# Cross entropy with label smoothing: a first row in three transfers, a second row in eleven, eight of which follow into its buffers

## The chip, the cores and the metric

The kernel runs on one core of a Trainium2 chip. The metric is the device time of one execution in microseconds (us). A profiled execution also has a span, from its first to its last instruction; here it is some 1.8 to 2.2 us shorter than the time.

The engines are named as in the profile: PE multiplies matrices, ACT computes exponentials and logarithms, DVE is the vector engine, POOL is the general engine beside it, and SP issues most of the loads. SBUF and PSUM are the two on-chip memories in which the tiles lie. At the end PE turns the 128 results of a row into one line (a transpose); matmuls without a use of their own, the "warming" ones, run before the last two transposes.

## The reference

```python
batch, num_classes = 256, 32000          # logits float32, labels int32, smoothing 0.1
log_probs = logits - max(logits, axis=-1)
log_probs = log_probs - log(sum(exp(log_probs), axis=-1))
targets   = smoothing / num_classes everywhere, plus 1 - smoothing at the label
out       = -sum(targets * log_probs, axis=-1)        # 256 values
```

256 rows on 128 partitions are two rows per partition, "row 0" and "row 1". For each row the kernel needs the sum of the logits (DVE), the sum of their exponentials (ACT), the label's logit (a gather), and at the end a logarithm. All 32.77 MB must be loaded once.

## The kernel before

A row is loaded in tiles. DVE and ACT both work on a tile when it has landed. DVE sums the first and second half in one instruction with two inputs; ACT writes its exponentials to a scratch tile that nobody reads and keeps the sum, which a second short instruction (ACTIVATION_READ_ACCUMULATOR) then writes out.

```python
WIDTHS = (
    (8000, 8000, 8000, 8000),
    (8000, 6272, 4736, 3648, 2688, 2048, 1536, 1216, 1024, 832),
)
TURN_MAX = 3648
...
    def sum_logits(xt, w: int, out: bass.AP):
        h = w // 2
        jd = junk.tile([P, max(WIDTHS[0]) // 2], FP32, name="jd", tag="jd")
        return nc.vector.scalar_tensor_tensor(
            out=jd[:, :h], in0=xt[:, :h], scalar=1.0, in1=xt[:, h:w],
            op0=ALU.mult, op1=ALU.add, accum_out=out)

    def sum_exps(xt, w: int, out: bass.AP) -> None:
        if w > TURN_MAX:
            ja = junk.tile([P, max(WIDTHS[0])], BF16, name="ja", tag="ja")   # one scratch tile
        else:
            ja = turn.tile([P, TURN_MAX], BF16, name="jt", tag="jt")         # three in turn
        nc.scalar.activation(out=ja[:, :w], in_=xt[:, :w], func=AF.Exp, accum_out=out)
...
        # after row 0: halve the partial sums on POOL until one is left, then the logarithm on ACT
        while n > 1:
            n //= 2
            half = small.tile([P, 2, n], FP32, ...)
            nc.gpsimd.tensor_tensor(out=half[:], in0=sums[:, :, :n], in1=sums[:, :, n:], op=ALU.add)
            sums = half
        nc.scalar.activation(out=lse[:], in_=sums[:, 1, :], func=AF.Ln)
...
    elast = psum.tile([P, 1], FP32, name="elast", tag="elast")   # row 1: sum of the last tile
    ...
    nc.scalar.activation(out=lse[:], in_=elast[:], func=AF.Ln, bias=done[2][:, 1:2])
```

The softmax here doesn't subtract the row's maximum and nothing guards it: scores larger than these inputs give would overflow.

Of the kernel before, what the change touches and what calls it, by code (L numbers as in the profile page):

```python
# [8 lines left out]
FP32 = mybir.dt.float32  # L9
BF16 = mybir.dt.bfloat16  # L10
I32 = mybir.dt.int32
ALU = mybir.AluOpType
AF = mybir.ActivationFunctionType
# [1 line left out]


WIDTHS = (
    (8000, 8000, 8000, 8000),
    (8000, 6272, 4736, 3648, 2688, 2048, 1536, 1216, 1024, 832),
)  # L20

RING_MIN = 4736

TURN_MAX = 3648

WARM_LEFT, WARM_COLS = 5, 256

# [32 lines left out]
def kernel(  # L60
# [7 lines left out]
    nc = tc.nc  # L68
    nc.at_finalize(_issue_first_transfers_at_start)
    B, C = logits.shape  # L70
    P = nc.NUM_PARTITIONS
    R = B // P
# [4 lines left out]
    c_small = eps / float(C)  # L77
    c_big = 1.0 - eps

    ring = ctx.enter_context(tc.tile_pool(name="ring", bufs=3))  # L80
    tail = ctx.enter_context(tc.tile_pool(name="tail", bufs=1))
    junk = ctx.enter_context(tc.tile_pool(name="junk", bufs=1))
    turn = ctx.enter_context(tc.tile_pool(name="turn", bufs=3))
    small = ctx.enter_context(tc.tile_pool(name="small", bufs=1))

    psum = ctx.enter_context(
        tc.tile_pool(name="psum", bufs=1, space=bass.MemoryType.PSUM)
    )

    tbl = _exp_ln_table(nc.m.arch)  # L90
    if tbl is not None:
        nc.scalar.add_instruction(  # L92
            mybir.InstLoadActFuncSet(
                name=nc.get_next_instruction_name(),
# [7 lines left out]
    x = logits.rearrange("(p r) c -> p (r c)", r=R)  # L102
# [3 lines left out]
        out=lab[:], in_=labels.bitcast(I32).rearrange("(p f) -> p f", p=P)  # L106
    )
    rowoff = small.tile([P, R], I32, name="rowoff", tag="rowoff")
    for r in range(R):
        nc.gpsimd.iota(  # L110
            out=rowoff[:, r : r + 1],
# [6 lines left out]
        out=flat_idx[:],  # L118
        in0=rowoff[:],
        in1=lab[:].rearrange("p (r two) -> p r two", two=2)[:, :, 0:1],  # L120
        op=ALU.add,
    )
    gat = small.tile([P, R], FP32, name="gat", tag="gat")
    for r in range(R):
        nc.gpsimd.indirect_dma_start(  # L125
            out=gat[:, r : r + 1],
            out_offset=None,
            in_=logits[:],
# [12 lines left out]
    weighted = [  # L141
        small.tile([P, 1], FP32, name=f"weighted{r}", tag=f"weighted{r}")[:]
        for r in range(R - 1)
    ] + [xsum[:, 0:1]]
    for r in range(R):
        nc.gpsimd.tensor_scalar(  # L146
            out=weighted[r],
            in0=gat[:, r : r + 1],
# [4 lines left out]

    res = small.tile([1, P, R], FP32, name="res", tag="res")

    def load(w: int, col: int, name: str):
        if w >= RING_MIN:
            xt = ring.tile([P, max(WIDTHS[0])], FP32, name="xt", tag="xt")
        else:
            xt = tail.tile([P, w], FP32, name=name, tag=name)  # L160
        if col == 0:

            h = w // 2
            nc.sync.dma_start(out=xt[:, :h], in_=x[:, :h])
            nc.scalar.dma_start(out=xt[:, h:w], in_=x[:, h:w])
        else:
            nc.sync.dma_start(out=xt[:, :w], in_=x[:, col : col + w])  # L167
        return xt

    def sum_logits(xt, w: int, out: bass.AP):  # L170
# [3 lines that stand above are left out]
            out=jd[:, :h],  # L174
            in0=xt[:, :h],
            scalar=1.0,
            in1=xt[:, h:w],
            op0=ALU.mult,
            op1=ALU.add,
            accum_out=out,  # L180
        )

    def sum_exps(xt, w: int, out: bass.AP) -> None:
        if w > TURN_MAX:
            ja = junk.tile([P, max(WIDTHS[0])], BF16, name="ja", tag="ja")
        else:
            ja = turn.tile([P, TURN_MAX], BF16, name="jt", tag="jt")
        nc.scalar.activation(out=ja[:, :w], in_=xt[:, :w], func=AF.Exp, accum_out=out)  # L188

    def row_of(column: bass.AP, name: str):  # L190

        row = psum.tile([1, P], FP32, name=name, tag=name)
        nc.tensor.transpose(out=row[:], in_=column, identity=ident[:])  # L193
        return row

    col = 0
    for r in range(R - 1):
        n = len(WIDTHS[r])
        sums = small.tile([P, 2, n], FP32, name=f"sums{r}", tag=f"sums{r}")
        for t, w in enumerate(WIDTHS[r]):  # L200
            xt = load(w, col, f"xl{r}_{t}")
            col += w
            sum_logits(xt, w, sums[:, 0, t : t + 1])
            sum_exps(xt, w, sums[:, 1, t : t + 1])


        while n > 1:
            assert n % 2 == 0
            n //= 2
            half = small.tile([P, 2, n], FP32, name=f"half{r}_{n}", tag=f"half{r}_{n}")  # L210
            nc.gpsimd.tensor_tensor(  # L211
                out=half[:], in0=sums[:, :, :n], in1=sums[:, :, n:], op=ALU.add
            )
            sums = half
        lse = small.tile([P, 1], FP32, name=f"lse{r}", tag=f"lse{r}")
        nc.scalar.activation(out=lse[:], in_=sums[:, 1, :], func=AF.Ln)  # L216
        lin = small.tile([P, 1], FP32, name=f"lin{r}", tag=f"lin{r}")
        nc.gpsimd.tensor_tensor(out=lin[:], in0=sums[:, 0, :], in1=weighted[r], op=ALU.add)
        scaled = small.tile([P, 1], FP32, name=f"scaled{r}", tag=f"scaled{r}")
        nc.gpsimd.tensor_scalar(  # L220
            out=scaled[:], in0=lin[:], scalar1=-c_small, scalar2=None, op0=ALU.mult
        )
        loss = small.tile([P, 1], FP32, name=f"loss{r}", tag=f"loss{r}")
        nc.gpsimd.tensor_tensor(out=loss[:], in0=scaled[:], in1=lse[:], op=ALU.add)  # L224
        loss_t = row_of(loss[:], f"loss_t{r}")
        nc.vector.tensor_copy(out=res[:, :, r : r + 1], in_=loss_t[:])  # L226
# [2 lines left out]

    r = R - 1  # L230
    n = len(WIDTHS[r])
    elast = psum.tile([P, 1], FP32, name="elast", tag="elast")
    pairs = [
        small.tile([P, 2], FP32, name=f"pair{i}", tag=f"pair{i}") for i in range(2)
    ]
# [3 lines left out]
    warm = psum.tile([P, WARM_COLS], FP32, name="warm", tag="warm")  # L239
    for t, w in enumerate(WIDTHS[r]):  # L240
        left = n - 1 - t
        xt = load(w, col, f"xl{r}_{t}")
        col += w
        part = sum_logits(
            xt, w, xsum[:, t + 1 : t + 2] if left > 1 else pairs[1 - left][:, 0:1]
        )
        if left == 0:
            sum_exps(xt, w, elast[:])
        elif left <= 2:
            sum_exps(xt, w, pairs[2 - left][:, 1:2])  # L250
        else:
            sum_exps(xt, w, esum[:, t : t + 1])
        if left == 2:
            with tc.issue_after(part.ins):
                nc.vector.tensor_reduce(
                    out=done[0][:, 0:1], in_=xsum[:, : t + 2], axis=AX.X, op=ALU.add
                )
                nc.vector.tensor_reduce(
                    out=done[0][:, 1:2], in_=esum[:, :t], axis=AX.X, op=ALU.add
                )  # L260
        elif left < 2:
            i = 1 - left
            nc.vector.tensor_tensor(  # L263
                out=done[i + 1][:], in0=done[i][:], in1=pairs[i][:], op=ALU.add
            )
        if left == WARM_LEFT:


            for i in range(w // WARM_COLS):
                nc.tensor.matmul(  # L270
                    warm[:],
                    lhsT=ident[:],
                    rhs=xt[:, i * WARM_COLS : (i + 1) * WARM_COLS],
                    start=True,
                    stop=True,
                )

    lse = small.tile([P, 1], FP32, name=f"lse{r}", tag=f"lse{r}")
# [6 lines left out]
        out=res[:, :, r : r + 1],  # L285
        in0=lin_row[:],
        scalar=-c_small,
        in1=lse_t[:],
# [4 lines left out]
        out=out.rearrange("(g i) -> g i", g=1), in_=res[:].rearrange("g p r -> g (p r)")  # L293
# [36 lines left out]
```

## Time and profile before

| What | Value |
|---|---|
| Time, median | 84.79 us (84.74 to 84.87, 6 runs) |
| Span of the profiled run | 83.2 us |
| Busy: ACT, DVE, POOL | 58.8, 37.1, 5.7 us |
| Idle of ACT before the first tile of row 1 | 1.75 us |
| Start of the last logarithm | 80.20 us |

The prediction below shows the chain of waits and ACT's timeline. The lines of a timeline give start, duration, engine, line, operation, tiles, and in brackets how long the engine had been idle and who released it.

```profile
45.07 0.08 DVE L173 DVE_READ_ACCUMULATOR jd<-xt 128x1 f32 x1
...
47.85 0.20 POOL L211 TENSOR_TENSOR half<-sums 128x4 f32<-128x4 f32 x1 [28.18 <-ACT ja L188]
48.12 0.19 POOL L211 TENSOR_TENSOR half<-half 128x2 f32<-128x2 f32 x1
```

DVE had finished its tile at 45.15 and didn't start the next before 50.32 (but for a small copy at 49.62). POOL's additions, 0.20 and 0.19 us, fall in that pause, so their durations are those of a POOL beside which DVE does nothing.

### The profile page before, as it was taken

The numbers are of one execution on the slowest core, as the hardware profiler recorded it, in microseconds if no ns is written. First come the engines' busy times: TensorE is split into PE (matmuls) and PEld (weight loads), VectorE is DVE, ScalarE is ACT, GpSimd is POOL, SyncE is SP. The second block draws the span as 40 slices with busy tenths as digits, with TensorE's granted clock in tenths as the row PEclk, the third lists the DMA queues.
The fourth block names the chain that finished last, engine by engine and source line by source line (L and its number), as shares of the span: only waits on it lengthen the run. The fifth ranks groups of instructions, "written<-read, shape, count | busy, mean of one in ns | idle before, by whom it ended". The sixth has DMA issues, their size and how long they took to land.

```text
span 83.2 us, 230 instructions
## 1 busy us (share of the span) xinstructions
PE 7.0 (8%) x23; PEld 5.0 (6%) x23; DVE 37.1 (45%) x35; ACT 58.8 (71%) x31; POOL 5.7 (7%) x19
## 2 busy tenths in 40 slices
PE   0000000000000000000000010000000000899020
PEld 0000000000000000000000000000000000787000
DVE  0000005950495009910397017922944736754860
ACT  5000005997499809994399908997999999999960
POOL 3201640031000000000000040000000000000000
PEclk9999999999999999999999999999999999999995
DMA  5999999997999899989998998998999999999600
GB/s 131 416 416 408 454 423 462 477 447 323 477 493 431 369 431 493 446 369 416 493 462 354 416 439 386 495 447 370 428 420 414 442 407 415 412 414 412 256 0 0
DMA packets 2258, 32.77 MB, mean 394 GB/s; under 512 B 337, under 2 KB 338, under 8 KB 850
## 3 DMA queue, kind: packets, MB, share of 16 engines
q1 hardware_dynamic: 2018, 30.72, 87.4%
q10 hardware_dynamic: 144, 2.05, 5.8%
q0 software_dynamic: 96, 0.00, 0.1%
HBM read 32.77 MB, written 0.00 MB: 394 GB/s over the span
## 4 chain that ended last, share of the span: by engine, by line
DMA 64%; ACT 32%; issue 1%; SPq 0%; PE 0%; DVE 0%; ACTq 0%
DMA xt<-in_logits_dram 40%; DMA xl<-in_logits_dram 23%; ACT ja L188 17%; ACT jt L188 15%; SPq L167 0%; PE lse_t L193 0%; DVE res L284 0%; ACT lse L279 0%; ACTq L188 0%
## 5 line engine op out<-in xcount | busy, mean ns | idle before, releaser
L188 ACT ACTIVATE ja<-xt 128x8000 bf16<-128x8000 f32 (+2 forms) x7 | 43.9, 6276 | 20.1 <-DMA xt<-in_logits_dram 20.0
L173 DVE SCALAR_TENSOR_TENSOR jd<-xt 128x4000 f32<-128x4000 f32 (+2 forms) x7 | 27.7, 3954 | 33.6 <-DMA xt<-in_logits_dram 33.6
L188 ACT ACTIVATE jt<-xl 128x3648 bf16<-128x3648 f32 (+6 forms) x7 | 12.2, 1748 | 0.1
L173 DVE SCALAR_TENSOR_TENSOR jd<-xl 128x1824 f32<-128x1824 f32 (+6 forms) x7 | 7.9, 1125 | 5.2 <-DMA xl<-in_logits_dram 5.0
L270 PE MATMUL warm<-xl,ident 128*128 128x256 f32 x20 | 6.1, 471 | 21.4 <-DMA xl<-in_logits_dram 21.4
L270 PEld LDWEIGHTS warm<-xl,ident 128*128 128x128 f32 x20 | 4.8, 246 | 22.5 <-DMA xl<-in_logits_dram 21.7
L193 PE MATMUL loss_t<-ident,loss 128*1 128x128 f32 x1 | 0.4, 372 | 49.2 <-POOL loss L224 49.2
L193 PEld LDWEIGHTS loss_t<-ident,loss 128*1 128x1 f32 x1 | 0.1, 79 | 49.2 <-POOL loss L224 49.2
L226 DVE COPY res<-loss_t 1x128 f32<-1x128 f32 x1 | 0.3, 278 | 4.5 <-PE loss_t L193 4.5
L211 POOL TENSOR_TENSOR half<-sums 128x4 f32<-128x4 f32 x1 | 0.2, 198 | 28.2 <-ACT ja L188 28.2
L125 POOL DMA_INDIRECT gat<-in_logits_dram,flat_idx x2 | 2.0, 1004 | 0.7 <-POOL ident masks.py:199 0.4
L92 ACT ACT_TABLE_LOAD x1 | 1.3, 1283 | 0.9 <-PEq L311 0.9
L188 ACT ACTIVATION_READ_ACCUMULATOR ja<-xt 128x1 f32 x7 | 1.3, 186 | 0.0
L188 ACT ACTIVATION_READ_ACCUMULATOR jt<-xl 128x1 f32 x7 | 1.3, 181 | 0.0
L146 POOL TENSOR_SCALAR weighted<-gat 128x1 f32<-128x1 f32 x1 | 0.8, 763 | 5.8 <-DMA gat<-in_logits_dram,flat_idx 5.8
L105 POOL DMA_DIRECT2D lab<-in_labels_dram x1 | 0.8, 766 | 1.0 <-POOLq L311 1.0
L216 ACT ACTIVATE lse<-half 128x1 f32<-128x1 f32 x1 | 0.2, 203 | 0.6 <-POOL half L211 0.6
L173 DVE DVE_READ_ACCUMULATOR jd<-xt 128x1 f32 x7 | 0.6, 82 | 0.0
L173 DVE DVE_READ_ACCUMULATOR jd<-xl 128x1 f32 x7 | 0.6, 82 | 0.0
L117 POOL TENSOR_TENSOR flat_idx<-rowoff,lab 128x2 int32<-128x2 int32 x1 | 0.2, 197 | 5.4 <-DMA lab<-in_labels_dram 5.4
L193 PE MATMUL lin_t<-ident,done 128*1 128x128 f32 x1 | 0.3, 270 | 3.0 <-DVE done L263 3.0
L282 DVE COPY lin_row<-lin_t 1x128 f32<-1x128 f32 x1 | 0.3, 278 | 0.4 <-PE lin_t L193 0.4
(20 smaller groups left out, 3.8 us busy)
## 6 DMA issues: line engine op xcount, KB each, us to landing
xt<-in_logits_dram SPq DMA_DIRECT2D x4, 4000.0 KB, 21.1
xt<-in_logits_dram SPq DMA_DIRECT2D x1, 3136.0 KB, 19.4
xt<-in_logits_dram SPq DMA_DIRECT2D x1, 2368.0 KB
xt<-in_logits_dram SPq DMA_DIRECT2D x1, 2000.0 KB, 11.5
xt<-in_logits_dram ACTq DMA_DIRECT2D x1, 2000.0 KB, 13.2
xl<-in_logits_dram SPq DMA_DIRECT2D x1, 1824.0 KB, 19.5
xl<-in_logits_dram SPq DMA_DIRECT2D x1, 1344.0 KB, 22.3
xl<-in_logits_dram SPq DMA_DIRECT2D x1, 1024.0 KB, 24.3
```

What stands on the lines that cost most here:

```text
L92: nc.scalar.add_instruction(mybir.InstLoadActFuncSet(name=nc.get_next_instruction_name(), act_func_set_id=tbl, ins=[], outs=[],))
L105: nc.gpsimd.dma_start(out=lab[:], in_=labels.bitcast(I32).rearrange("(p f) -> p f", p=P))
L117: nc.gpsimd.tensor_tensor(out=flat_idx[:], in0=rowoff[:], in1=lab[:].rearrange("p (r two) -> p r two", two=2)[:, :, 0:1], op=ALU.add,)
L125: nc.gpsimd.indirect_dma_start(out=gat[:, r : r + 1], out_offset=None, in_=logits[:], in_offset=bass.IndirectOffsetOnAxis(ap=flat_idx[:, r ...
L146: nc.gpsimd.tensor_scalar(out=weighted[r], in0=gat[:, r : r + 1], scalar1=label_weight, scalar2=None, op0=ALU.mult,)
L173: return nc.vector.scalar_tensor_tensor(out=jd[:, :h], in0=xt[:, :h], scalar=1.0, in1=xt[:, h:w], op0=ALU.mult, op1=ALU.add, accum_out=out,)
L188: nc.scalar.activation(out=ja[:, :w], in_=xt[:, :w], func=AF.Exp, accum_out=out)
L193: nc.tensor.transpose(out=row[:], in_=column, identity=ident[:])
L211: nc.gpsimd.tensor_tensor(out=half[:], in0=sums[:, :, :n], in1=sums[:, :, n:], op=ALU.add)
L226: nc.vector.tensor_copy(out=res[:, :, r : r + 1], in_=loss_t[:])
L270: nc.tensor.matmul(warm[:], lhsT=ident[:], rhs=xt[:, i * WARM_COLS : (i + 1) * WARM_COLS], start=True, stop=True,)
L282: nc.vector.tensor_copy(out=lin_row[:], in_=lin_t[:])
```

## The change

Row 0 comes in three larger transfers, row 1 in eleven, of which eight go into parts of row 0's buffers; a chain of additions replaces the halving; the last sum lies in SBUF. The intent is presumably a load stream of fewer, longer transfers at the start and a shorter last tile.

```diff
-    (8000, 8000, 8000, 8000),
-    (8000, 6272, 4736, 3648, 2688, 2048, 1536, 1216, 1024, 832),
+    (8576, 11712, 11712),
+    (7040, 6656, 4800, 3520, 2624, 1984, 1536, 1216, 1024, 832, 768),
-RING_MIN = 4736
-TURN_MAX = 3648
+FOLLOW = (1, 2, 5)      # how many tiles of row 1 go into each buffer of row 0
+TURN_MAX = 2624
 ...
+            buf = wide.tile([P, w], FP32, name=f"wide{b}_{r}", tag=f"wide{b}")
+            for v in widths:
+                buffers.append(buf[:, at : at + v])
+                at += v
 ... (the last three tiles of row 1 have buffers of their own)
-        while n > 1:  ... halving on POOL ...
+        total = sums[:, :, 0:1]
+        for t in range(1, n):
+            acc = small.tile([P, 2, 1], FP32, ...)
+            nc.gpsimd.tensor_tensor(
+                out=acc[:], in0=total, in1=sums[:, :, t : t + 1], op=ALU.add)
+            total = acc[:]
-        nc.scalar.activation(out=lse[:], in_=sums[:, 1, :], func=AF.Ln)
+        nc.scalar.activation(out=lse[:], in_=total[:, 1, :], func=AF.Ln)
 ...
-    elast = psum.tile([P, 1], FP32, name="elast", tag="elast")
+    elast = small.tile([P, 1], FP32, name="elast", tag="elast")
```

More of the change, by code (lines that the diff above doesn't have):

```diff
@@ L78 @@
     c_big = 1.0 - eps
-    ring = ctx.enter_context(tc.tile_pool(name="ring", bufs=3))
+    wide = ctx.enter_context(tc.tile_pool(name="wide", bufs=1))
     tail = ctx.enter_context(tc.tile_pool(name="tail", bufs=1))
@@ L154, with load @@
     res = small.tile([1, P, R], FP32, name="res", tag="res")
-    def load(w: int, col: int, name: str):
-        if w >= RING_MIN:
-            xt = ring.tile([P, max(WIDTHS[0])], FP32, name="xt", tag="xt")
-        else:
-            xt = tail.tile([P, w], FP32, name=name, tag=name)
+    assert R == 2 and len(FOLLOW) == len(WIDTHS[0])
+    buffers = []
+    for r in range(R):
+        for b, w in enumerate(WIDTHS[0]):
+            widths = WIDTHS[0][b : b + 1]
+            if r == 1:
+                t = sum(FOLLOW[:b])
+                widths = WIDTHS[1][t : t + FOLLOW[b]]
+            buf = wide.tile([P, w], FP32, name=f"wide{b}_{r}", tag=f"wide{b}")
+            assert sum(widths) <= w
+            at = 0
+            for v in widths:
+                buffers.append(buf[:, at : at + v])
+                at += v
+    for t in range(sum(FOLLOW), len(WIDTHS[1])):
+        w = WIDTHS[1][t]
+        buffers.append(tail.tile([P, w], FP32, name=f"tail{t}", tag=f"tail{t}")[:])
+    def load(w: int, col: int):
+        xt = buffers.pop(0)
         if col == 0:
@@ L166, in load @@
         else:
-            nc.sync.dma_start(out=xt[:, :w], in_=x[:, col : col + w])
+            nc.sync.dma_start(out=xt, in_=x[:, col : col + w])
         return xt
@@ L200 @@
         for t, w in enumerate(WIDTHS[r]):
-            xt = load(w, col, f"xl{r}_{t}")
+            xt = load(w, col)
             col += w
@@ L204 @@
             sum_exps(xt, w, sums[:, 1, t : t + 1])
-        while n > 1:
-            assert n % 2 == 0
-            n //= 2
-            half = small.tile([P, 2, n], FP32, name=f"half{r}_{n}", tag=f"half{r}_{n}")
+        total = sums[:, :, 0:1]
+        for t in range(1, n):
+            acc = small.tile([P, 2, 1], FP32, name=f"acc{r}_{t}", tag=f"acc{r}_{t}")
             nc.gpsimd.tensor_tensor(
-                out=half[:], in0=sums[:, :, :n], in1=sums[:, :, n:], op=ALU.add
+                out=acc[:], in0=total, in1=sums[:, :, t : t + 1], op=ALU.add
             )
-            sums = half
+            total = acc[:]
         lse = small.tile([P, 1], FP32, name=f"lse{r}", tag=f"lse{r}")
-        nc.scalar.activation(out=lse[:], in_=sums[:, 1, :], func=AF.Ln)
+        nc.scalar.activation(out=lse[:], in_=total[:, 1, :], func=AF.Ln)
         lin = small.tile([P, 1], FP32, name=f"lin{r}", tag=f"lin{r}")
-        nc.gpsimd.tensor_tensor(out=lin[:], in0=sums[:, 0, :], in1=weighted[r], op=ALU.add)
+        nc.gpsimd.tensor_tensor(out=lin[:], in0=total[:, 0, :], in1=weighted[r], op=ALU.add)
         scaled = small.tile([P, 1], FP32, name=f"scaled{r}", tag=f"scaled{r}")
@@ L241 @@
         left = n - 1 - t
-        xt = load(w, col, f"xl{r}_{t}")
+        xt = load(w, col)
         col += w
```

## The prediction

> **What bounds the kernel now.** I read the chain that ended last first, because shares of busy time (ACT 71%, DVE 45%) say nothing of who sets the end. The chain, from the page of the kernel before and then piece by piece:
>
> ```profile
> DMA 64%; ACT 32%; issue 1%; SPq 0%; PE 0%; DVE 0%; ACTq 0%
> ...
> 20.35 20.37 DMA xt<-in_logits_dram
> ...
> 48.17 19.52 DMA xl<-in_logits_dram
> 67.69 0.02 issue
> 67.72 7.63 ACT jt L188 x5
> 75.34 0.04 issue
> 75.39 1.47 ACT jt L188
> ...
> 80.20 0.27 ACT lse L279
> ```
>
> The load stream sets the time up to 67.7 us and ACT's exponentials after it. The second view is the timeline of ACT, to see whether ACT waits for data in that tail (columns: start, duration, then what runs):
>
> ```profile
> 40.80 6.87 ACT L188 ACTIVATE ja<-xt 128x8000 bf16<-128x8000 f32 x1 [2.51 <-DMA xt<-in_logits_dram]
> 47.58 0.19 ACT L188 ACTIVATION_READ_ACCUMULATOR ja<-xt 128x1 f32 x1
> 48.35 0.20 ACT L216 ACTIVATE lse<-half 128x1 f32<-128x1 f32 x1 [0.58 <-POOL half L211]
> 50.31 6.87 ACT L188 ACTIVATE ja<-xt 128x8000 bf16<-128x8000 f32 x1 [1.75 <-DMA xt<-in_logits_dram]
> ...
> 67.72 3.24 ACT L188 ACTIVATE jt<-xl 128x3648 bf16<-128x3648 f32 x1
> 70.86 0.19 ACT L188 ACTIVATION_READ_ACCUMULATOR jt<-xl 128x1 f32 x1
> 70.96 2.44 ACT L188 ACTIVATE jt<-xl 128x2688 bf16<-128x2688 f32 x1
> ...
> 79.24 0.88 ACT L188 ACTIVATE jt<-xl 128x832 bf16<-128x832 f32 x1
> 80.02 0.15 ACT L188 ACTIVATION_READ_ACCUMULATOR jt<-xl 128x1 f32 x1
> 80.20 0.26 ACT L279 ACTIVATE lse<-elast,done 128x1 f32<-128x1 f32 x1
> ```
>
> The reader is to see two things. ACT idles 1.75 to 2.5 us before each big tile, so its work there is hidden behind loading; and 67.72 + 3.24 = 70.96, so in the tail one ACTIVATE starts where the last one ends. DVE, in its own timeline, still waits 0.55 to 1.7 us for data in the tail. So loads and ACT run in lockstep there: the falling widths make each exponential last as long as the next load. Nothing can be won by speeding up one alone.
>
> Third, is the load stream ever short of work? The table of queues and the slices of the page:
>
> ```profile
> DMA  5999999997999899989998998998999999999600
> q1 hardware_dynamic: 2018, 30.72, 87.4%
> ```
>
> No. The dips are packet records ending in bursts. The starts on ACT and DVE that a landing releases give a straight line: 8000 columns take 9.48 us (21.84 to 31.33), 6272 take 7.46, 2048 take 2.49, 1216 take 1.51. Fitted by me: 0.072 us per transfer + 1.1768 ns per column (512 bytes, so 435 GB/s), with an effective start at 2.86 us. It returns the landings 21.83, 31.32, 40.81, 50.29, 57.74, 63.39, 67.76, 70.99 ... 79.18, within 0.1 us of the trace.
>
> **What the Trainium skill says.** "DMA: Bandwidth & Descriptors", section Where 436 GB/s comes from, puts the ceiling of the path into SBUF at 435.2 GB/s; the fit's slope is 435, so the stream has no rate left to gain. "ScalarE: Activation LUTs", section What ACT_TABLE_LOAD costs, gives an ACTIVATE as 186 ns + 0.833 ns per element, about 93 ns more for a pointer operand. The trace agrees on slope: 8000 columns 6870 ns, 1024 columns 1057 ns, which is 203 + 0.8333 ns per column. The same page, section Step-by-step, says that writing PSUM from ScalarE is lower in latency than writing SBUF: here reading the accumulator took 149 ns into PSUM against 186 into SBUF, so the trace agrees. "TensorE: Matmul & The Clock Gate", section Part 1, says the array's clock halves after an idle window of some 3.4 us; here a transpose took 372 ns after a long idle time and 270 ns after the warming matmuls.
>
> **The change part by part.**
>
> 1. Loads. Transfers in the stream: 4 + 10 before, 3 + 11 after, again 14, and the same bytes. By the fit the last column lands at 79.18 us both times. Row 0 ends one transfer earlier, at 40.73 in place of 40.81: 0.07 us, paid back in row 1. Expected gain: 0.
>
> 2. Do the loads still come in time? A later load waits until DVE and ACT have left the buffer. Buffer 0 (8576 columns, landed near 14) is free near 21.5; its successor is not needed before 40.73. Buffer 1 lands at 26.88, free near 37.0, needed at 49.09. Buffer 2 lands at 40.73, free near 50.8, needed at 62.72. The queue always holds at least one more transfer. Reuse of completion counters also delays issue (before, the last load was issued only at 57.70, after the 6272-column tile landed): that makes the last load wait for the 4800-column tile at 62.7, far ahead of its turn at 78.2. No cost.
>
> 3. ACT at the turn of the rows. This is where the time changes. Before, the last tile of row 0 had 8000 columns and ACT idled 1.75 us before row 1. Now it has 11712: 0.203 + 9.760 = 9.96 us from 40.73, so it ends at 50.69. Then the pool engine's one addition (two before, but one already hidden) and the logarithm: from the end of the ACTIVATE 0.18 us to POOL, 0.23 more to the logarithm (one step of the two that took 47.67 to 48.35), 0.20 for it. ACT is free at 51.31, while the first tile of row 1 has landed at 49.09. ACT is 2.2 us behind and has no idle time left.
>
> 4. ACT through row 1. Eleven ACTIVATEs: 11 x 0.203 + 32000 x 0.8333 ns = 2.23 + 26.67 = 28.90 us, so it ends at 80.20 if nothing stalls. Step by step every tile has landed 0.2 to 0.4 us before ACT gets to it, so ACT alone now sets the tail. Before, the last ACTIVATE ended at 79.24 + 0.88 = 80.12: +0.08.
>
> 5. A stall on the scratch output. The 7040, 6656, 4800 and 3520 columns are over the limit of 2624, so all four write the one wide scratch tile, where each must wait for the previous one's completion; narrower ones rotate over three. That this wait exists shows in the count of waits on ACT: 11 of 14 tiles had an extra one, which is 1 (two halves) + 6 (wide scratch reused) + 4 (rotation reused). Before it was hidden, as the wide tiles waited for data. Its size, an estimate: the accumulator's read ends 0.09 us after the ACTIVATE (70.96 against 70.86 + 0.19), and from a release to a start take another 0.09 (13.28 to 13.37). So 0.18 us for each of three transitions: +0.54.
>
> 6. The last sum in SBUF. Accumulator read 186 in place of 149, the logarithm perhaps 0.28 in place of 0.26: +0.06.
>
> 7. Warming matmuls. They hang on the sixth-last tile, now 1984 columns: 14 matmuls in place of 20, from about 72.5. In the trace the granted clock fell to half at about 80.85, just after the last transpose ended at 80.80. A transpose near 81.3 probably meets the low clock: 0.10 us, counted at 0.6: +0.06.
>
> Sum: 0.08 + 0.54 + 0.06 + 0.06 = +0.74; as the 0.18 in step 5 is the least certain term, I shade it to about +0.6, hence 85.4 us, 0.7% slower.
>
> **The rivals.** First: the scratch stall doesn't exist or costs little, since the same engine runs in order. Then +0.1 to +0.2, 85.0 us. For it: the rotating tiles with an extra wait (78.18 + 1.06 = 79.24) start without a gap. Against it: those wait for an instruction three back.
> Second: loads into parts of one buffer wait for compute on the neighbouring part. Then the five tiles in buffer 2 would load and compute in turn, 5 us or more lost, about 90 us. Against it: the two gathers into one tile were issued at 8.93 and 10.28 although the first result was used only at 17.03, so parts are tracked separately. I give it 3%.
> Third: larger transfers do stream better, by more than the fit's 0.07 us, as was presumably intended. Even so ACT's chain from 40.73 sets the end; only an earlier landing of row 0's last tile moves it. 0.3 us earlier would make the result equal, 84.8.
>
> **Range and chances.** Terms 3 and 4 are sums of measured durations, good to 0.1 us; step 5 spans 0 to 0.6, step 7 0 to 0.1. So 84.75 to 85.9. Two per cent is 1.7 us: slower by that needs the second rival (4%), faster would need ACT to end before 78.5, though it holds 38.9 us of work after 40.7 (1%).
>
> **What would show it.** Right: ACT idle before the first tile of row 1 gone; no wait of ACT for data after about 41 us; 0.1 to 0.2 us between ACTIVATEs on the wide scratch and none among the narrow ones; the chain naming ACT from about 40.7 to the end; last landing still near 79.2. Wrong: ACT waiting for data in row 1, waits of SP on ACT between parts of one buffer, or row 0's last tile starting well before 40.7.

## The result, and the profile after

The changed kernel takes 87.27 us (87.24 to 87.44, 6 runs) against 84.79 before: the ratio is 1.0295, with a 95% interval of 1.0282 to 1.0309. The ratios here differ from the ratio of the medians by about 0.001 at most. It is slower by 2.5 us, where 0.6 was forecast and 85.9 was the upper end of the range.

The chain of waits of the changed kernel, by engine, is the line to be careful with:

```profile
DMA 79%; ACT 16%; issue 1%; PE 0%; DVE 0%; ACTq 0%
```

It was DMA 64% and ACT 32% before, as if loading had become the trouble. It had not. The end of the stream shows in two half microseconds of each trace (window, its length, busy time of PE, weight loads, DVE, ACT, POOL, then clock, DMA share and GB/s), before and after:

```profile
78.00:78.50 0.50, 0.00 (x0) 0.00 (x0) 0.38 (x1) 0.50 (x3) 0.00 (x0) 1.00 0.50 193
78.50:79.00 0.50, 0.00 (x0) 0.00 (x0) 0.40 (x3) 0.50 (x1) 0.00 (x0) 1.00 0.02 7
```

```profile
78.00:78.50 0.50, 0.00 (x0) 0.00 (x0) 0.01 (x1) 0.50 (x3) 0.00 (x0) 1.00 0.58 221
78.50:79.00 0.50, 0.00 (x0) 0.00 (x0) 0.00 (x0) 0.50 (x2) 0.00 (x0) 1.00 0.02 6
```

Both streams run dry in the first of the two. The last tile of row 0 lands at the same time too: ACT and DVE start on it at 40.80 before and at 40.83 after. A chain follows one releaser back at each step; where ACT had long been late, it still went by way of a load (up to 78.27, to the landing of the last one, though ACT had no pause there).

The timeline of the changed kernel at the turn of the rows shows where the time went:

```profile
40.83 9.96 ACT L204 ACTIVATE ja<-wide 128x11712 bf16<-128x11712 f32 x1 [3.80 <-DMA wide<-in_logits_dram]
...
49.20 3.82 DVE L189 SCALAR_TENSOR_TENSOR jd<-wide 128x3520 f32<-128x3520 f32 x1 [2.09 <-DMA wide<-in_logits_dram]
50.70 0.19 ACT L204 ACTIVATION_READ_ACCUMULATOR ja<-wide 128x1 f32 x1
51.02 2.06 POOL L225 TENSOR_TENSOR acc<-acc,sums 128x2 f32<-128x2 f32 x1 [13.71 <-ACT ja L204]
52.95 0.08 DVE L189 DVE_READ_ACCUMULATOR jd<-wide 128x1 f32 x1
53.11 0.20 ACT L230 ACTIVATE lse<-acc 128x1 f32<-128x1 f32 x1 [2.22 <-POOL acc L225]
...
53.22 6.05 ACT L204 ACTIVATE ja<-wide 128x7040 bf16<-128x7040 f32 x1
```

POOL adds two columns on 128 partitions, and it takes 2.06 us in place of 0.19. DVE began the sum of row 1's first tile at 49.20 and ended it at 53.02; POOL's addition ends at 53.08. ACT, which needs the addition for the logarithm, stands idle for 2.22 us. From 53.22 on ACT goes through eleven tiles without once waiting for data, so nothing of that is made up. The rest of its timeline:

```profile
59.40 5.75 ACT L204 ACTIVATE ja<-wide 128x6656 bf16<-128x6656 f32 x1
...
65.27 4.20 ACT L204 ACTIVATE ja<-wide 128x4800 bf16<-128x4800 f32 x1
...
69.60 3.14 ACT L204 ACTIVATE ja<-wide 128x3520 bf16<-128x3520 f32 x1
...
72.73 2.37 ACT L204 ACTIVATE jt<-wide 128x2624 bf16<-128x2624 f32 x1
...
82.48 0.29 ACT L293 ACTIVATE lse<-elast,done 128x1 f32<-128x1 f32 x1
```

Between wide tiles there are gaps: 59.40 + 5.75 = 65.15, but the next starts at 65.27. After the last wide one there is none: 69.60 + 3.14 = 72.74, and the next starts at 72.73. The three gaps (0.13, 0.12, 0.13) are 0.38 us together.

The last logarithm starts 2.28 us later than before (82.48 against 80.20), which is nearly the whole growth of the span (85.5 against 83.2).

### The profile page after: what moved, and what is told of

The parts are those of the page before. It is cut to its first block, busy times and chain, and to the rows that moved or that the text cites. A ratio compares the mean times of both kernels' runs of the same rounds, so it can differ in the third digit from the quotient of the medians. Undisturbed runs are those within 1.5% of the kernel's fastest.

```text
span 85.5 us, 218 instructions
## 1 busy us (share of the span) xinstructions
PE 6.0 (7%) x17; PEld 4.1 (5%) x17; DVE 36.9 (43%) x35; ACT 58.4 (68%) x31; POOL 8.0 (9%) x19
## 4 chain that ended last, share of the span: by engine, by line
DMA 79%; ACT 16%; issue 1%; PE 0%; DVE 0%; ACTq 0%
DMA wide<-in_logits_dram 54%; DMA tail<-in_logits_dram 25%; ACT ja L204 12%; ACT jt L204 4%; ACT lse L293 0%; PE lse_t L209 0%; DVE res L298 0%; ACTq L204 0%
## 5 line engine op out<-in xcount | busy, mean ns | idle before, releaser
L204 ACT ACTIVATE ja<-wide 128x11712 bf16<-128x11712 f32 (+5 forms) x7 | 46.4, 6632 | 21.2 <-DMA wide<-in_logits_dram 21.1
L189 DVE SCALAR_TENSOR_TENSOR jd<-wide 128x5856 f32<-128x5856 f32 (+9 forms) x11 | 33.7, 3064 | 41.4 <-DMA wide<-in_logits_dram 41.4
L204 ACT ACTIVATE jt<-wide 128x2624 bf16<-128x2624 f32 (+3 forms) x4 | 6.9, 1719 | 0.0
L284 PE MATMUL warm<-wide,ident 128*128 128x256 f32 x14 | 5.0, 535 | 18.2 <-DMA wide<-in_logits_dram 18.2
L284 PEld LDWEIGHTS warm<-wide,ident 128*128 128x128 f32 x14 | 3.8, 282 | 19.4 <-DMA wide<-in_logits_dram 18.5
L225 POOL TENSOR_TENSOR acc<-acc,sums 128x2 f32<-128x2 f32 x1 | 2.1, 2056 | 13.7 <-ACT ja L204 13.7
L204 ACT ACTIVATE jt<-tail 128x1024 bf16<-128x1024 f32 (+2 forms) x3 | 2.7, 915 | 0.0
L189 DVE SCALAR_TENSOR_TENSOR jd<-tail 128x512 f32<-128x512 f32 (+2 forms) x3 | 1.8, 609 | 0.5 <-DMA tail<-in_logits_dram 0.5
L204 ACT ACTIVATION_READ_ACCUMULATOR ja<-wide 128x1 f32 x7 | 1.3, 186 | 0.0
L189 DVE DVE_READ_ACCUMULATOR jd<-wide 128x1 f32 x11 | 0.9, 82 | 0.0
```

The source lines that it names most:

```text
L189: return nc.vector.scalar_tensor_tensor(out=jd[:, :h], in0=xt[:, :h], scalar=1.0, in1=xt[:, h:w], op0=ALU.mult, op1=ALU.add, accum_out=out,)
L225: nc.gpsimd.tensor_tensor(out=acc[:], in0=total, in1=sums[:, :, t : t + 1], op=ALU.add)
L284: nc.tensor.matmul(warm[:], lhsT=ident[:], rhs=xt[:, i * WARM_COLS : (i + 1) * WARM_COLS], start=True, stop=True,)
```

## The experiments

The theory after the first look: POOL's addition is locked out of SBUF by the DVE instruction, because that instruction has two inputs from SBUF, and the changed order of events has put the two at the same time. The Trainium skill says as much: "SBUF — State Buffer", section Who interferes with whom, has DVE's second input come through a read interface that it shares with GpSimd, so that a DVE instruction with two SBUF inputs and a GpSimd (POOL) instruction that reads SBUF exclude each other, while a DVE instruction with at most one SBUF input does not disturb, unless it runs in one of the modes that use two ports. The trace agrees on the 2.06 us, but a coincidence of times is no proof. The rivals are that any DVE work blocks POOL, that POOL is slow by itself at that time, and that the large last tile makes ACT late with or without the addition.

All kernels below gave correct results. The kernel before, run beside each, had medians of 84.81 to 84.83 us. The changed kernel was not run again beside them; a difference from its 87.27 us is one between sessions, and it is the kernel before (84.79 then) that ties them together.

### One input in place of two

```diff
-        part = sum_logits(xt, w, xsum[:, t + 1 : t + 2] ...)
+        if t == 0:
+            nc.vector.tensor_reduce(out=xsum[:, 1:2], in_=xt[:, :w], axis=AX.X, op=ALU.add)
+        else:
+            part = sum_logits(xt, w, xsum[:, t + 1 : t + 2] ...)
```

> The changed kernel, but the sum over the first tile of the second row (7040 columns) is one reduction with a single input from SBUF, in place of the instruction that reads two halves. DVE is then busy for some 7.4 us (49.2 to 56.6), longer than before. Theory (the pool engine's addition is locked out by a DVE instruction with two inputs from SBUF until that ends): the addition falls from 2.06 to about 0.2 us, the logarithm starts at about 51.2 in place of 53.11, and the kernel takes 87.27 - 1.9 = 85.4 us. Rival 1 (any DVE work blocks the pool engine): the addition lasts about 5.5 us and the kernel takes about 90.5 us. Rival 2 (the addition is slow by itself at that time, after a long pause or beside the load stream): 2.06 us and 87.3 us stay.

Measured: 85.73 us (4 runs), ratio to before 1.0101 (1.0084 to 1.0117). DVE and POOL in this kernel's timeline:

```profile
49.14 7.49 DVE L259 TENSOR_REDUCE xsum<-wide 128x1 f32<-128x7040 f32 x1 [2.02 <-DMA wide<-in_logits_dram]
...
51.03 0.19 POOL L225 TENSOR_TENSOR acc<-acc,sums 128x2 f32<-128x2 f32 x1 [13.71 <-ACT ja L204]
```

DVE is busy for twice as long around the addition, and the addition takes 0.19 us. Rivals 1 and 2 both fall. ACT is free at 51.36 in place of 53.22, 1.86 us earlier, and the span shrinks by 1.9 us to 83.6. The time shrank by only 1.5; the missing part lies outside the span (see the last points below).

### One input with a full output

The reduction also dropped the wide result. So the same was tried with two one-input instructions that write one:

```diff
+        if t == 0:
+            for k, at in enumerate((1, n - 1)):      # two halves of 3520 columns
+                nc.vector.tensor_scalar(
+                    out=jd[:, :h], in0=xt[:, k * h : (k + 1) * h], scalar1=1.0, scalar2=0.0,
+                    op0=ALU.mult, op1=ALU.add, accum_out=xsum[:, at : at + 1])
```

> The first run (one input) changed two things: the reduction reads one stream in place of two, and it writes one column in place of a 3520-column result. Here the sum over the first tile of the second row is two DVE instructions of 3520 columns, each with one input from SBUF and a full 3520-column output beside the accumulated sum; the first lasts about 3.8 us from 49.2, so the pool engine's addition falls inside it. Theory (the second input is what locks the pool engine out): the addition takes 0.2 us and the kernel 85.4 to 85.8 us, as in the run with the reduction. Rival (the wide output locks it out): the addition ends with the first instruction, near 53, lasts 2 us, and the kernel takes 87.3 us.

Measured: 85.59 us (4 runs), ratio 1.0091 (1.0070 to 1.0113).

```profile
49.13 3.82 DVE L262 TENSOR_SCALAR_CACHE_REDUCE jd<-wide 128x3520 f32<-128x3520 f32 x1 [2.11 <-DMA wide<-in_logits_dram]
...
50.92 0.19 POOL L225 TENSOR_TENSOR acc<-acc,sums 128x2 f32<-128x2 f32 x1 [13.71 <-ACT ja L204]
```

This instruction has the same start (to 0.07 us), the same 3.82 us and the same output as the one in the changed kernel. It differs in operation and in having one input, and POOL passes freely. With the run before it, neither DVE being busy nor the output keeps POOL out; what is left is the two-input instruction. That it is its second input, and not something else of this operation, was not tested apart (no run had another two-input operation beside the addition, or this one with an input outside SBUF); there the page of the skill is what speaks for the input.

### A shorter two-input instruction

```diff
+CUT = 4800
+        if t == 0:
+            sum_logits(xt[:, :CUT], CUT, xsum[:, 1:2])      # the other 2240 columns after tile 1
```

> The changed kernel, but the two-input sum over that first tile is cut: 4800 of its columns at once (about 2.66 us, 49.20 to 51.86), the other 2240 after the second tile's sum. Theory: the addition ends where the shortened instruction ends, near 51.95, so it lasts about 0.9 us in place of 2.06, and the kernel takes 87.27 - 1.15 = 86.1 us. Rival 2 (slow by itself): 2.06 us and 87.3 us. Rival 1 gives the same as the theory here.

Measured: 86.30 us (86.01 to 86.51, 4 runs), ratio 1.0171 (1.0141 to 1.0201).

```profile
49.07 2.66 DVE L191 SCALAR_TENSOR_TENSOR jd<-wide 128x2400 f32<-128x2400 f32 x1 [2.09 <-DMA wide<-in_logits_dram]
...
50.89 0.89 POOL L227 TENSOR_TENSOR acc<-acc,sums 128x2 f32<-128x2 f32 x1 [13.71 <-ACT ja L206]
```

DVE's instruction now ends at 51.73 and POOL's at 51.78; the addition lasts 0.89 us, as forecast. Cut the instruction by 1.16 us, and the wait shrinks by 1.17. POOL waits for the end of the whole instruction.

### No POOL between ACT and ACT

```diff
-        nc.scalar.activation(out=lse[:], in_=total[:, 1, :], func=AF.Ln)
+        nc.scalar.activation(out=lse[:], in_=sums[:, 1, n - 1 : n], func=AF.Ln,
+                             bias=before_last[:, 1, :])       # the sum of the tiles before it
```

> The changed kernel, but the logarithm of the first row takes the last partial sum as input and the sum of the others as its bias, so no addition of the pool engine lies between ACT and ACT; the pool engine still adds for the linear part. Theory: the logarithm starts at about 50.95, ACT is free at about 51.2 in place of 53.2, and the kernel takes 87.27 - 2.0 = 85.3 us, though the pool engine's addition is as long as ever (about 2 us). Rival 3 (the large last tile of the first row alone makes ACT late, wait or no wait): 87.0 us or more.

Measured: 85.25 us (85.11 to 85.42, 4 runs), ratio 1.0053 (1.0032 to 1.0073), as the theory had it.

```profile
50.91 0.29 ACT L231 ACTIVATE lse<-sums,acc 128x1 f32<-128x1 f32 x1
50.95 2.06 POOL L226 TENSOR_TENSOR acc<-acc,sums 128x2 f32<-128x2 f32 x1 [13.72 <-ACT ja L204]
```

The addition is still locked out for as long, but nobody on the path waits for it, and 2.0 us come back. The large last tile alone (rival 3) isn't the cause.

### The small tile of row 0 last

```diff
-    (8576, 11712, 11712),
+    (11712, 11712, 8576),
-FOLLOW = (1, 2, 5)
+FOLLOW = ((0, 3), (1, 2), (4, 5, 6, 7))      # which tiles of row 1 go into which buffer
```

> The changed kernel with the first row's widths in another order, 11712, 11712, 8576 (and the buffers of the second row's tiles dealt out to fit). Same transfers, bytes and instructions. Theory: ACT ends the last tile at about 48.3 and the addition runs at 48.4 to 48.6, before DVE starts at 49.2, so it lasts 0.2 us; ACT waits for data again before the second row, and the kernel takes about 84.9 us (the stall of about 0.12 us between exponentials on the wide scratch is then mostly hidden or adds 0.1 to 0.2). Rival 2 (slow by itself): the addition stays at 2 us, ACT free at about 50.7, and the kernel takes about 85.0 us too, so the duration of the addition tells here, not the time.

Measured: 85.12 us (84.97 to 85.49, 4 runs), ratio 1.0037 (1.0003 to 1.0070).

```profile
48.66 0.20 POOL L225 TENSOR_TENSOR acc<-acc,sums 128x2 f32<-128x2 f32 x1 [7.42 <-ACT ja L204]
...
49.45 6.07 ACT L204 ACTIVATE ja<-wide 128x7040 bf16<-128x7040 f32 x1 [0.35 <-DMA wide<-in_logits_dram]
```

The same transfers in another order: the addition runs while DVE has no tile, takes 0.20 us, and ACT waits for data again. So it is the order, that the tile ACT needs longest for comes just before the turn, that brought the two instructions together. The same trace has the exclusion in a larger dose: POOL's operation on one column of gathered logits, which took 0.76 us in the kernel before, starts at 17.34 beside DVE's two-input instruction on the first 11712 columns (17.18 to 23.44) and takes 6.18 us. The time is 0.2 us over the forecast; in this profile row 0's last tile started at 41.09 in place of 40.83.

### Two scratch tiles in turn, and one for all

```diff
-        if w > TURN_MAX: ja = junk.tile(... "ja")      # one wide scratch tile
-        else:            ja = turn.tile(... "jt")
+        k = scratch.pop(0)                             # row 1: 1, 0, 1, 0, ...
+        ja = junk.tile([P, SCRATCH[k]], BF16, name=f"ja{k}", tag=f"ja{k}")
```

> The changed kernel, but the exponentials of the second row write two scratch tiles in turn, so none writes where the one before it wrote. Theory (an exponential must wait for the completion of the one before it when both write the same scratch tile, 0.125 us at each of the three transitions between the wide tiles): the gaps between the end of one ACTIVATE and the start of the next fall from about 0.12 to 0 and the kernel takes 87.27 - 0.38 = 86.9 us. Rival (the gaps come from the tiles' width or from semaphore traffic): gaps and time stay.

Measured: 86.82 us (86.66 to 86.94, 5 runs), ratio 1.0225 (1.0204 to 1.0245), so 0.45 us faster than the changed kernel.

```profile
59.28 5.73 ACT L203 ACTIVATE ja<-wide 128x6656 bf16<-128x6656 f32 x1
...
65.01 4.19 ACT L203 ACTIVATE ja<-wide 128x4800 bf16<-128x4800 f32 x1
```

59.28 + 5.73 = 65.01: the gap is gone, and the ACTIVATEs themselves are 0.01 to 0.02 us shorter. The opposite dose sets the limit for the rotating tiles to 0, so that all eleven tiles write the one wide scratch tile:

> The opposite: all eleven exponentials of the second row write the one wide scratch tile, so seven more transitions must wait. Theory: each of the ten gaps is about 0.125 us, and the kernel takes 87.27 + 7 x 0.125 = 88.15 us. Rival: narrow tiles keep a gap of 0, 87.3 us.

Measured: 88.21 us (88.19 to 88.48, 5 runs), ratio 1.0397 (1.0377 to 1.0416), 0.94 us slower than the changed kernel where 0.88 was expected.

```profile
77.50 1.48 ACT L203 ACTIVATE ja<-wide 128x1536 bf16<-128x1536 f32 x1
...
79.10 1.22 ACT L203 ACTIVATE ja<-wide 128x1216 bf16<-128x1216 f32 x1
```

Narrow tiles now have the gap too (77.50 + 1.48 = 78.98, next start 79.10). The stall belongs to writing the scratch tile again, at 0.12 to 0.13 us each, and not to width.

### The last sum in PSUM

```diff
-    elast = small.tile([P, 1], FP32, name="elast", tag="elast")
+    elast = psum.tile([P, 1], FP32, name="elast", tag="elast")
```

> The changed kernel with the last sum of exponentials in PSUM, as before the change. Expected from the two traces: the accumulator's read 0.15 in place of 0.19 us and the logarithm 0.26 in place of 0.29, so 87.27 - 0.06 = 87.2 us; a rival that the place costs nothing gives 87.27.

Measured: 87.15 us (87.13 to 87.54, 5 runs), ratio 1.0278 (1.0255 to 1.0302). In its timeline the read of the accumulator takes 0.15 us in place of 0.19, and the logarithm 0.26 in place of 0.29: 0.07 us together, as expected. The times don't resolve it, since the interval overlaps that of the changed kernel. Nor does the span (85.5 both times): in this profile the two last transposes took 0.37 us each in place of 0.27.

### All three costs out, and two attempts at a better kernel

The bias, the two scratch tiles and PSUM together, with the widths of the changed kernel:

> The changed kernel with its own widths in both rows, and all three found costs taken away: logarithm of the first row with a bias, two scratch tiles in turn, last sum in PSUM. Theory: the costs add up, 2.0 + 0.38 + 0.06, so 87.27 - 2.4 = 84.85 us, level with the kernel before; ACT's last exponential then begins about when its data lands. If something else of the change costs time, the kernel stays above 85.2 us.

Measured: 84.90 us (84.79 to 85.10, 6 runs), ratio 1.0007 (0.9988 to 1.0025): level with the kernel before. Two lines from its timeline:

```profile
74.34 1.48 ACT L203 ACTIVATE ja<-wide 128x1536 bf16<-128x1536 f32 x1
74.35 0.96 DVE L188 SCALAR_TENSOR_TENSOR jd<-wide 128x768 f32<-128x768 f32 x1 [0.70 <-DMA wide<-in_logits_dram]
```

ACT and DVE start on the same tile within 0.01 us, when it lands: ACT is in step with the loads again. Taken away singly, the three costs gave 2.02, 0.45 and 0.12 us, together 2.37, a little less than their sum, as ACT cannot get ahead of the loads. The three costs account for the whole loss, and with them gone the new tiling neither gains nor loses.

To beat both, the ten tiles of the kernel before were put behind a row 0 of three, one transfer fewer. First with the small tile last:

> A version meant to beat both: first row 11712, 11712, 8576, the second row in the ten tiles of the kernel before, following into the first row's buffers; logarithm of the first row with a bias in place of the pool engine's addition, two scratch tiles in turn, last sum in PSUM. Thirteen transfers in place of fourteen. Theory: every wait that was found is gone, ACT is again in step with the loads, and the last landing is one fixed cost of a transfer (0.07 us) earlier than in the kernel before: 84.7 to 84.8 us, at most 0.1% faster than before. If loading has no such fixed cost: 84.8 us.

Measured: 85.14 us (85.04 to 86.04, 6 runs), ratio 1.0049 (1.0013 to 1.0086). Two runs lie near 86.0; the profiled one is one of them, and there row 0's last tile started at 41.48, 0.65 us late. Then with the small tile first:

> As the run with all waits out, with the first row still 8576, 11712, 11712 but the second row in the ten tiles of the kernel before (8000 to 832), following into the first row's buffers. Thirteen transfers in place of fourteen, one fixed cost of 0.07 us less. Theory: 84.75 us, at most 0.1% faster than before, so not to be told from it for sure; the slow start of the loads seen where the first tile has 11712 columns should not be there.

Measured: 85.17 us (85.07 to 85.34, 6 runs), ratio 1.0037 (1.0019 to 1.0055). Neither beats the kernel before. In the profile of the second the late start is indeed not there (40.71), and its span is 83.1 us, like that of the kernel with all waits out; yet its time is 0.27 us longer.

What stays open: why a first tile of 11712 columns lands late, and why in some of these kernels (the one with the reduction, the last two, and three runs of four of the kernels with two one-input instructions and with the shorter two-input one) 1.9 to 2.2 us of the time lie outside the span, in place of some 1.8. No run was aimed at either.

## Why the prediction was wrong, by its own steps

**Steps 1 and 2 (loads) held.** Same end of the stream, row 0 in at 40.83 against 40.73 forecast, and every load issued in time: SP issued the five loads into the third buffer one after another, from 50.91 to 53.14. So the second rival, that parts of one buffer wait for each other, fell. The third, that long transfers stream better, fell as well: row 0 was not in any earlier.

**Step 3 failed, in the term of POOL's addition.** The prediction had ACT lose its idle time at the turn, which is right, and took "0.23 more to the logarithm" from the trace of before. There DVE was idle. The measured term is 2.09 us (51.02 to 53.11), 1.86 more, and ACT is free at 53.22 in place of 51.31. The step counted DVE's sum as work beside the path, though the same step's arithmetic says that DVE begins on row 1 at 49.1 and that ACT is done at 50.7, so that the addition must fall inside a DVE instruction. None of the rivals named it. ("Two before, but one already hidden" does not fit the kernel before either: there both additions, at 47.85 and 48.12, came after the ACTIVATE. It is in the changed kernel that the first of two is hidden, at 37.12. The sum does not suffer from it.) Take the 1.86 us off and 85.41 us is left, just what was forecast (the runs with this wait gone and the widths kept took 85.25 to 85.73). That it agrees so well is partly luck: steps 4 and 5 were together 0.30 too large, and 0.14 had been shaded off.

The sign of it was in the trace of before, in the very lines that the second rival quotes from (one at 17.03):

```profile
13.38 4.33 DVE L173 SCALAR_TENSOR_TENSOR jd<-xt 128x4000 f32<-128x4000 f32 x1 [13.38 <-DMA xt<-in_logits_dram]
...
17.03 0.76 POOL L146 TENSOR_SCALAR weighted<-gat 128x1 f32<-128x1 f32 x1 [5.79 <-DMA gat<-in_logits_dram,flat_idx]
...
19.46 0.21 POOL L146 TENSOR_SCALAR xsum<-gat 128x1 f32<-128x1 f32 x1 [1.67 <-DMA gat<-in_logits_dram,flat_idx]
```

Two equal operations on one column, 0.76 and 0.21 us. The long one ends at 17.79, just after DVE's instruction at 17.71. The same operation with two durations was the question to ask.

**Step 4 held but for 0.14 us.** ACT alone sets the tail, though the sign that was named for it, a chain that names ACT from about 40.7 to the end, did not come: that chain has loads from 37.06 to 78.27. Eight of the eleven ACTIVATEs cost 0.186 us beside their columns and not 0.203; the longer figure was read from ACTIVATEs that had waited.

**Step 5 was right in mechanism, too large in size.** Three gaps of 0.12 to 0.13 us, 0.38 together, in place of 0.54. The accumulator's read ends 0.10 us after the ACTIVATE (59.37 against 59.27), as reckoned, but the next ACTIVATE starts 0.03 us after that (59.40), not 0.09. Removing them and adding seven more moved the time as forecast; the first rival fell.

**Step 6 held** in the trace (0.07 us). **Step 7 did not happen here**: the last transpose took 0.27 us. It did in four of the ten profiles of kernels with 14 warming matmuls (0.37 us, in the two runs on scratch tiles, with the sum in PSUM and with all waits out), and in none of the three with 20. So the risk is real but not steady, and the pause of PE before the transposes does not tell the cases apart: 4.24 us here, 2.44 with all waits out.

The sum for the end of the last ACTIVATE: forecast 80.74, plus 1.91 at the turn, less 0.16 of the stall, less 0.14 of step 4, gives 82.35; measured 81.53 + 0.83 = 82.36.

## What to carry to other kernels

When a change moves an instruction in time, look at what the neighbours do at its new place: a duration read where an engine was alone holds only there, and two durations of one operation in a trace are the warning. Keep a POOL instruction out of a chain from ACT to ACT where DVE may be running two-input instructions, or give DVE one input there; here a bias on the logarithm replaced the addition at the price of 0.09 us (the logarithm took 0.29 in place of 0.20). Let outputs that nobody reads rotate over two tiles once the engine has no idle time, and trust a chain's shares less than the idle time before each instruction.

## What the Trainium skill lacked or had wrong

- On the main cause nothing was lacking. "SBUF — State Buffer" has the exclusion, which the prediction did not look up, and the runs agree: 6.18 us beside a two-input instruction of 6.26 us, 2.06 beside one of 3.82, 0.89 beside one of 2.66, and 0.19 beside one-input instructions of 3.82 and 7.49. It has to be looked up wherever POOL and DVE both work.
- "ScalarE: Activation LUTs" says nothing of back-to-back ACTIVATEs that write one scratch tile again: 0.12 to 0.13 us lost at each, none with two tiles in turn. Its 186 ns of fixed cost fits the ACTIVATEs that had not waited; in those that had, for a load or for the scratch tile, it was 203 ns.
- "DMA: Bandwidth & Descriptors" gives about 2.0 us as the fixed part of one transfer, fitted there to transfers issued from GpSimd (POOL). In this stream, queued by SP, the prediction's fit to the landings leaves 0.07 us for each; what a single transfer costs by itself no run here measured.
